# Two groups of gates and partners, and the last six feature blocks of a down product, as Strassen's seven products

## The chip, the cores and the metric

The kernel runs on one core of a Trainium2 chip. The metric is the device time of one execution in microseconds (us). The engines that matter here are TensorE (PE, the matmuls), VectorE (DVE), ScalarE (ACT) and the queue of DMA issues on SyncE (SP).

## The reference

Two decoder blocks over a sequence of 512 rows of width 1024, in float32. The first has latent and windowed attention and a plain feed-forward network, the second a convolution beside a dilated attention, and then this, which is where the change lies:

```python
    h = rmsnorm(x, g_ffn[i])
    gate = causal_dwconv3(h @ w_gate[i], ffn_conv_w[i], ffn_conv_b[i])
    x = x + (jax.nn.silu(gate) * (h @ w_up[i])) @ w_down[i]
    ple_gate = jax.nn.sigmoid(rmsnorm(x, g_ple[i]) @ w_ple_gate[i])
    x = x + ple_gate * (p[i].astype(x.dtype) @ w_ple_proj[i])
```

`w_gate` and `w_up` are 1024 x 2816 and `w_down` is 2816 x 1024. `causal_dwconv3` weighs each feature's row with the two rows before it.

## The kernel before

**Precision.** Every float32 operand is split into a rounded part `hi` (a cast on ACT) and a rest `lo` (a subtraction on DVE); `split` does both. `mm3` makes three matmuls of a pair of operands, hi·hi, hi·lo and lo·hi, into one PSUM bank. Weights come by DMA into raw tiles (`wr`, three slots, or `wq`, four) and are split into `wh` and `wl`, which have four slots of 1024 columns each. There are eight PSUM banks.

**Gates and partners.** The 2816 features are 22 blocks of 128 and 11 groups of two blocks. For a group, `gated(gr, 0)` makes the gate (banks `gp`) and `gated(gr, 1)` the partner from `w_up` (banks `up`): each 8 steps of 128 deep, two blocks, three matmuls of 128x512, 48 in all. `gate_ev` makes the convolution (ACT `y`, two dependent steps on DVE for each block) and the silu on ACT; `up_ev` multiplies with the partner. The products of groups 0 to 7 go into raw tiles `hr` (`RAW`, four blocks in one tile), those of groups 8 to 10 are split at once into `ah` and `al` (list `H`). Group 0 is made by `gated_first`, in an order that follows the arrival of the normalized tiles. Groups 1 to 3 follow, and then groups 4 to 10 stand between the products of the down calls.

**The down product.** The first 16 feature blocks go through `down_steps` in two calls of eight blocks. A call takes two raw tiles as a 2 x 2 matrix of operands (A11, A21, A12, A22) and four quarters of the weights (`wq`: B11, B22, B12, B21) and makes the seven products of the Strassen-Winograd scheme in place of eight: sums of the A's (`a_sum`), of the B's (`b_sum`), the split of each operand (`a_op` into `aop`, `b_op` into `wh`, `wl`), 24 matmuls of 512 columns per product into the banks `r`, and additions of the banks into `x` (`ev_add`). Its generator yields after every product, and a part of a gated group is made between two products.

**The last six blocks.** Blocks 16 to 21 are a plain product over 6 steps of 128: `gemm_tm` for the left half of the columns (`tm`), `gemm_tm_t` for the right (`tt`), which has 144 matmuls of 512 columns in all, and whose additions into `x` (`ev_down`) are followed, tile by tile of 128 rows, by `to_ple`: row weights `xn`, squares with a sum on ACT (`xs`), and the factor of the last norm (`rv`, `rr`, `rs`, `ra`, `ro`). `put_off` lets the transposes of `xn` (`pt` into `xth`, `xtl`) wait for a later `tick` of PE's program. The ple gate (`tt<-wh,xth`) and its sigmoid `sg` end the kernel. In front of it stands the projection of `p_2` (`pt` of `pin`, `ptp`, `tm<-wh,ptp`, copies to `pp`).

**Order.** Each engine runs its instructions in one order, which a scheduler has laid down by priorities (`tc.high_priority`, with the offsets `A_PRIO` for the A operands, `B_PRIO` for the B operands and `W_PRIO` for weights).

Of the kernel before, what the change touches and what calls it, by code (L numbers as in the profile page):

```python
# [26 lines left out]
W_PRIO = 60  # L27
# [17 lines left out]

WEAVE = (-1, -1, -1, 0, -1, 1, -1, -1, 2, -1, 3)
A_PRIO, B_PRIO = 120, 80
MLA_WO_AT = (0, 0, 21, 23)


@with_exitstack
def tile_hybrid_decoder(ctx: ExitStack, tc: tile.TileContext, io: dict, out: bass.AP):
# [195 lines left out]
    def krows(W, k0, kn, c0, n):  # L248
        return W[k0 * P:(k0 + kn) * P, c0:c0 + n].rearrange("(k p) c -> p k c", p=P)
# [339 lines left out]
    with ExitStack() as mla:  # L589
# [300 lines left out]

    ts2 = slice(0, 256), slice(256, 512)

    def down_steps(mb, wd, row, ra, rb, alpha, after=None):


        A11, A21, A12, A22 = ra[:, :, ts2[0]], ra[:, :, ts2[1]], rb[:, :, ts2[0]], rb[:, :, ts2[1]]
        B = {}
        for r, h in ((0, 0), (1, 1), (0, 1), (1, 0)):
            n_big[0] += 1
            B[r, h] = q = mb.tile([P, 4, S], F32, tag="q", name=f"wq_{n_big[0]}")  # L900
            for i in range(2):
                nc.sync.dma_start(out=q[:, 2 * i:2 * i + 2, :],
                                  in_=krows(wd, row + r * 4 + 2 * i, 2, h * 512, 512))
        B11, B12, B21, B22 = B[0, 0], B[0, 1], B[1, 0], B[1, 1]

        def a_op(src):
            o = big("aop")
            hl = o.rearrange("p k c -> p (k c)").rearrange("p (f k c) -> p f k c", f=2, k=4)
            with tc.high_priority(offset=A_PRIO):
                split(hl[:, 0], hl[:, 1], src)  # L910
            return hl

        def a_sum(out, a, b, op):
            with tc.high_priority(offset=A_PRIO):
                nc.vector.tensor_tensor(out=out, in0=a, in1=b, op=op)

        def b_sum(out, a, b, op):
            with ExitStack() as es:
                es.enter_context(tc.high_priority(offset=A_PRIO))
                if after:  # L920
                    es.enter_context(tc.issue_after(after))
                for i in range(2):
                    ks = slice(2 * i, 2 * i + 2)
                    nc.vector.tensor_tensor(out=out[:, ks, :], in0=a[:, ks, :], in1=b[:, ks, :], op=op)  # L924

        def b_op(src):
            res = []
            for i in range(2):
                n_big[0] += 1
                wh = wp.tile([P, 1024], F32R, tag="wh", name=f"wh_{n_big[0]}")  # L930
                wl = wp.tile([P, 1024], F32R, tag="wl", name=f"wl_{n_big[0]}")
                with tc.high_priority(offset=B_PRIO):
                    split(wh, wl, src[:, 2 * i:2 * i + 2, :].rearrange("p k c -> p (k c)"))
                res.append([t.rearrange("p (k c) -> p k c", k=2) for t in (wh, wl)])
            return res

        def product(R, a, b, start):
            for i, (wh, wl) in enumerate(b):
                for tb in range(2):
                    for k in range(2):  # L940
                        ts_ = slice(tb * P, (tb + 1) * P)
                        kk = 2 * i + k
                        mm3(R[tb], (a[:, 0, kk, ts_], a[:, 1, kk, ts_]), (wh[:, k, :], wl[:, k, :]),
                            start and kk == 0, kk == 3)

        def add(R, th, h, al=1.0):
            for tb in range(2):
                ev_add(x, al)(h, 2 * th + tb, R[tb])

        def banks2(n):  # L950
# [48 lines left out]
        yield  # L999

    def mlp_ln(xt_in, x, l, first, nxt, rms=False):

# [567 lines left out]
    X = xt[2]  # L1570
    wg, wu, wd = io["w_gate_2"][0], io["w_up_2"][0], io["w_down_2"][0]
    with pool("ff", 2) as ff:
        H = []

        RAW = {}
        Y = {}

# [15 lines left out]
                nc.scalar.activation(y, y, AF.Silu)  # L1593

        def up_ev(gr, banks):
            if gr < 8 and gr % 2 == 0:
                RAW[gr // 2] = big("hr", F32)
            elif gr % 2 == 0:
                hh, hl = big("ah"), big("al")
                H.extend((hh[:, m, :], hl[:, m, :]) for m in range(4 if gr < 10 else 2))  # L1600
            for m in range(2):
                if gr < 8:
                    turned["y", gr] = nc.vector.tensor_tensor(
                        out=RAW[gr // 2][:, gr % 2 * 2 + m, :], in0=Y.pop((gr, m)), in1=banks[m], op=ALU.mult).ins
                    continue
                n_big[0] += 1
                a = ff.tile([P, S], F32, tag="a", name=f"a_{n_big[0]}")
                nc.vector.tensor_tensor(out=a, in0=Y.pop((gr, m)), in1=banks[m], op=ALU.mult)
                split(*H[gr * 2 + m - 16], a)
# [155 lines left out]
```

## Time and profile before

| | us |
|---|---|
| median of 3 runs | 1692.81 (1691.04 to 1693.84) |
| profiled execution | 1690.43 |
| its span | 1688.6 |
| PE busy in it | 1669.5 |
| DVE busy | 1111.0 |
| ACT busy | 829.3 |

The span is the part of the profiled execution between the first and the last instruction. Engines work side by side; matmuls are pipelined, so the start of one to the start of the next is what one costs in a stream, and not the time between its start and its end.

### The profile page before, as it was taken

The numbers are of one execution on the slowest core, as the hardware profiler recorded it, in microseconds if no ns is written. First come the engines' busy times: TensorE is split into PE (matmuls) and PEld (weight loads), VectorE is DVE, ScalarE is ACT, GpSimd is POOL, SyncE is SP. The second block draws the span as 40 slices with busy tenths as digits, with TensorE's granted clock in tenths as the row PEclk, the third lists the DMA queues.
The fourth block names the chain that finished last, engine by engine and source line by source line (L and its number), as shares of the span: only waits on it lengthen the run. The fifth ranks groups of instructions, "written<-read, shape, count | busy, mean of one in ns | idle before, by whom it ended". The sixth has DMA issues, their size and how long they took to land.

```text
span 1688.6 us, 21336 instructions
## 1 busy us (share of the span) xinstructions
PE 1669.5 (99%) x8239; PEld 1384.7 (82%) x8239; DVE 1111.0 (66%) x1938; ACT 829.3 (49%) x1416; POOL 25.6 (2%) x43
## 2 busy tenths in 40 slices
PE   8999999999999999999999999999999999999998
PEld 8777898888888877798888888988779888888887
DVE  5876648576846578738586846556765567577463
ACT  4665445444543578445444545444854343344442
POOL 0000000000001110000000000001000000000000
PEclk9999999999999999999999999999999999999999
DMA  5213244333132323413333143133352323422321
GB/s 181 69 46 130 88 150 119 100 100 100 50 125 87 101 63 119 156 50 101 101 99 100 50 126 111 39 125 99 100 187 63 88 76 99 125 63 63 113 88 63
DMA packets 125015, 165.22 MB, mean 98 GB/s; under 512 B 9385, under 2 KB 80322, under 8 KB 124914
## 3 DMA queue, kind: packets, MB, share of 16 engines
q1 hardware_dynamic: 119072, 150.03, 28.2%
q10 hardware_dynamic: 4626, 10.94, 1.9%
q0 software_dynamic: 1216, 2.89, 0.8%
q8 instruction: 65, 1.06, 0.3%
q14 instruction: 36, 0.29, 0.1%
HBM read 160.95 MB, written 2.88 MB: 97 GB/s over the span
## 4 chain that ended last, share of the span: by engine, by line
PE 94%; DVE 3%; ACT 1%; DMA 1%; issue 0%; SPq 0%; ACTq 0%; DVEq 0%
PE up L202 8%; PE up L204 8%; PE up L203 8%; PE r L202 6%; PE r L204 6%; PE r L203 6%; PE tt L203 3%; PE tt L204 3%; PE tt L202 3%; PE tm L202 2%; PE tm L203 2%; PE fm L202 2%; PE tm L204 2%; PE fm L203 2%; PE fm L204 2%; PE gp L204 2%
## 5 line engine op out<-in xcount | busy, mean ns | idle before, releaser
L120 DVE TENSOR_TENSOR wl<-wr,wh 128x1024 fp32r<-128x1024 f32 (+5 forms) x219 | 222.8, 1032 | 168.8 <-ACT wh L119 167.7
L119 ACT CAST wh<-wr 128x1024 fp32r<-128x1024 f32 (+5 forms) x219 | 193.6, 898 | 273.1 <-PE up L203 118.0
L202 PE MATMUL up<-xth,wh 128*128 128x512 f32 x608 | 236.5, 389 | 0.0
L203 PE MATMUL up<-xtl,wh 128*128 128x512 f32 x608 | 236.5, 389 | 0.0
L204 PE MATMUL up<-xth,wl 128*128 128x512 f32 x608 | 236.5, 389 | 0.0
L120 DVE TENSOR_TENSOR wl<-wq,wh 128x1024 fp32r<-128x1024 f32 x112 | 136.4, 1223 | 101.0 <-ACT wh L119 100.9
L119 ACT CAST wh<-wq 128x1024 fp32r<-128x1024 f32 x112 | 118.0, 1054 | 159.2 <-PE r L204 82.4
L204 PE MATMUL r<-wh,aop 128*128 128x512 f32 x448 | 174.3, 389 | 0.0
L202 PE MATMUL r<-wh,aop 128*128 128x512 f32 x448 | 174.3, 389 | 0.0
L203 PE MATMUL r<-wl,aop 128*128 128x512 f32 x448 | 174.3, 389 | 0.0
L204 PEld LDWEIGHTS up<-xth,wl 128*128 128x128 f32 x608 | 114.1, 188 | 23.8
L203 PEld LDWEIGHTS up<-xtl,wh 128*128 128x128 f32 x608 | 114.1, 188 | 23.6
L202 PEld LDWEIGHTS up<-xth,wh 128*128 128x128 f32 x608 | 114.1, 188 | 23.5
L204 PEld LDWEIGHTS r<-wh,aop 128*128 128x128 f32 x448 | 84.1, 188 | 17.5
L203 PEld LDWEIGHTS r<-wl,aop 128*128 128x128 f32 x448 | 84.1, 188 | 17.4
L202 PEld LDWEIGHTS r<-wh,aop 128*128 128x128 f32 x448 | 84.1, 188 | 17.4
L885 DVE SCALAR_TENSOR_TENSOR x<-x,r 128x512 f32<-128x512 f32 x144 | 92.5, 684 | 5.4 <-PE r L204 5.4
L120 DVE TENSOR_TENSOR aop<-hr,aop 128x1024 fp32r<-128x1024 f32 x56 | 67.0, 1221 | 21.5 <-ACT aop L119 21.5
L924 DVE TENSOR_TENSOR wq<-wq,wq 128x1024 f32<-128x1024 f32 x64 | 76.2, 1223 | 6.4 <-DMA wq<-in_w_down_dram 3.9
L202 PE MATMUL gp<-xth,wh 128*128 128x512 f32 x160 | 62.3, 389 | 0.0
L203 PE MATMUL gp<-xtl,wh 128*128 128x512 f32 x160 | 62.3, 389 | 0.0
L204 PE MATMUL gp<-xth,wl 128*128 128x512 f32 x160 | 62.2, 389 | 0.0
(426 smaller groups left out, 3561.4 us busy)
## 6 DMA issues: line engine op xcount, KB each, us to landing
wr<-in_mlp_w_up_dram SPq DMA_DIRECT2D x64, 512.0 KB, 3.8
wq<-in_mlp_w_down_dram SPq DMA_DIRECT2D x48, 512.0 KB, 4.3
wr<-in_w_in_dram SPq DMA_DIRECT2D x24, 512.0 KB, 3.6
wr<-in_w_gate_dram SPq DMA_DIRECT2D x22, 512.0 KB, 3.7
wr<-in_w_up_dram SPq DMA_DIRECT2D x22, 512.0 KB, 3.6
wr<-in_mlp_w_down_dram SPq DMA_DIRECT2D x16, 512.0 KB
wq<-in_w_down_dram SPq DMA_DIRECT2D x16, 512.0 KB, 7.8
wr<-in_mla_w_o_dram SPq DMA_DIRECT2D x8, 512.0 KB, 3.7
```

What stands on the lines that cost most here:

```text
L119: turned["hi"] = nc.scalar.copy(out=hi, in_=src).ins
L120: return nc.vector.tensor_tensor(out=lo, in0=src, in1=hi.bitcast(F32), op=ALU.subtract)
L202: nc.tensor.matmul(o, lhsT=sh, rhs=mh, start=start, stop=False, skip_group_check=True)
L203: nc.tensor.matmul(o, lhsT=sh, rhs=ml, start=False, stop=False, skip_group_check=True)
L204: nc.tensor.matmul(o, lhsT=sl, rhs=mh, start=False, stop=stop, skip_group_check=True)
L885: nc.vector.scalar_tensor_tensor(out=x[:, t, cs], in0=x[:, t, cs], scalar=alpha, in1=pb, op0=ALU.mult, op1=ALU.add)
L924: nc.vector.tensor_tensor(out=out[:, ks, :], in0=a[:, ks, :], in1=b[:, ks, :], op=op)
```

## The change

Two things are remade as seven products.

`gated_seven` makes the gate and the partner of groups 2 and 3 together. The operands are the four quarters of the normalized input (two halves of the depth, two halves of the 512 rows; `x_operands` makes the sums `s1` to `s4` of them once) and, as weights, the two halves of the depth of `w_gate` (B11, B21) and of `w_up` (B12, B22), in tiles `fq`. Each product is 24 matmuls of 128x256 into one bank, whose two halves are the group's two blocks; three banks take part, and `plus` on DVE adds the banks to the parts `fp` and `fv` (tile names with f: `fg` gate, `fu` partner).

The last six blocks go through `down_steps` with three steps of depth per quarter (`nk=3`) in place of four, with the last two products in reverse order (`fin`), so that `to_ple` is called for the tiles as they are complete. The six blocks stay in raw tiles, `RAW[4]` and `RAW[5]`, so `H` and its splits are gone. The loads of the ple gate's weights (`ahead2`) are issued between the products. In every call of `down_steps` the sum and the split of `s4` now stand ahead of the split of B21.

```diff
+SEVEN = 4
...
-    def down_steps(mb, wd, row, ra, rb, alpha, after=None):
+    def down_steps(mb, wd, row, ra, rb, alpha, after=None, nk=4, fin=None):
...
-            for i, (wh, wl) in enumerate(b):
+            for k0, kn, wh, wl in b:
                 for tb in range(2):
-                    for k in range(2):
+                    for k in range(kn):
...
+            tick()
...
-        b = b_op(B21)
-        product(R3, a22, b, False)
         a_sum(A12, A12, A22, ALU.subtract)
         s4 = a_op(A12)
-        add(R3, 1, 0)
-        yield
-        b = b_op(B22)
-        product(R2, s4, b, False)
-        add(R2, 0, 1)
-        yield
+        rest = [(R3, a22, B21, 1, 0), (R2, s4, B22, 0, 1)]
+        for R, a, src, th, h in reversed(rest) if fin else rest:
+            b = b_op(src)
+            product(R, a, b, False)
+            add(R, th, h, last=True)
+            yield
...
+            G, U = tmp("g", 2), tmp("u", 2)
+            p1, v = tmp("p"), tmp("v")
+            R1, R2, R3 = bank("gt"), bank("gt"), bank("gt")
+            product(R1, B11, "a11", True)
+            nc.scalar.copy(out=p1, in_=both(R1))
+            b_sum(B12, B22, B12, ALU.subtract)
+            product(R3, B12, "s3", True)
+            plus(v, p1, R3)
+            b_sum(B11, B12, B11, ALU.add)
+            product(R2, B11, "s2", True)
+            plus(G[:, :, ts2[1]], p1, R2)
+            product(R1, B21, "a12", False)
+            nc.scalar.copy(out=G[:, :, ts2[0]], in_=both(R1))
+            b_sum(B21, B21, B11, ALU.subtract)
+            product(R3, B21, "a22", False)
+            plus(G[:, :, ts2[1]], G[:, :, ts2[1]], R3)
+            gate_ev(gr, [G[:, m, :] for m in range(2)])
+            b_sum(B11, B22, B11, ALU.subtract)
+            product(R2, B11, "s1", False)
+            plus(U[:, :, ts2[1]], v, R2)
+            product(R2, B22, "s4", False)
+            plus(U[:, :, ts2[0]], p1, R2)
+            up_ev(gr, [U[:, m, :] for m in range(2)])
...
         gated_first()
-        for gr in range(1, 4):
+        ops = x_operands()
+        gated(1, 0)
+        gated(1, 1)
+        with pool("fm", 1) as fm:
+            for gr in range(2, SEVEN):
+                gated_seven(gr, fm, ops)
+        for gr in range(SEVEN, 4):
             for part in range(2):
                 gated(gr, part)
...
-        gemm_tm(H, wd[16 * P:22 * P, :], [LO], ev_down)
-        ahead2 = gemm_tm_t(H, wd[16 * P:22 * P, :], [HI], ev_down, 1,
-                           nxt=lambda: ahead_tm(io["w_ple_gate_2"][0], 0, 512))
+        with pool("fl", 4) as fl:
+            ahead2 = Ahead([(krows(io["w_ple_gate_2"][0], k, 2, 0, 512), 2, 512, None) for k in range(0, 8, 2)])
+            for i, _ in enumerate(down_steps(fl, wd, 16, RAW.pop(4)[:, 0:3, :], RAW.pop(5)[:, 0:3, :], 1.0, nk=3,
+                                             fin=to_ple)):
+                if 2 <= i < 6:
+                    ahead2.one()
```

**DVE at the end of the groups.** In the order of before, the last product with the partner of group 3 (`hr<-y,up`) and what follows it:

```order
L1324 SCALAR_TENSOR_TENSOR y_11869<-gp_11803,vec,y_11869 128x510
L120 TENSOR_TENSOR wl_12004<-wr_12002,wh_12003 128x1024
L1603 TENSOR_TENSOR hr_11799<-y_11864,up_11874 128x512
L1603 TENSOR_TENSOR hr_11799<-y_11869,up_11875 128x512
L120 TENSOR_TENSOR wl_12034<-wr_12032,wh_12033 128x1024
L120 TENSOR_TENSOR aop_12108<-hr_11799,aop_12108 128x1024
L915 TENSOR_TENSOR hr_11799<-hr_11799,hr_11526 128x4x256
L120 TENSOR_TENSOR wl_12075<-wq_11947,wh_12074 128x1024
```

In the order of the change, the same place; `wl_12179` is the first half of the first weights of the first down call:

```order
L1671 TENSOR_TENSOR fg_11933<-fg_11933,gt_11939 128x2x256
L1325 SCALAR_TENSOR_TENSOR y_12088<-fg_11933,vec,y_12088 128x511
L1325 SCALAR_TENSOR_TENSOR y_12093<-fg_11933,vec,y_12093 128x511
L1327 SCALAR_TENSOR_TENSOR y_12088<-fg_11933,vec,y_12088 128x510
L1327 SCALAR_TENSOR_TENSOR y_12093<-fg_11933,vec,y_12093 128x510
L1671 TENSOR_TENSOR fu_11934<-fv_11936,gt_11938 128x2x256
L1671 TENSOR_TENSOR fu_11934<-fp_11935,gt_11938 128x2x256
L1602 TENSOR_TENSOR hr_11922<-y_12088,fu_11934 128x512
L1602 TENSOR_TENSOR hr_11922<-y_12093,fu_11934 128x512
L121 TENSOR_TENSOR aop_12330<-hr_11922,aop_12330 128x1024
L916 TENSOR_TENSOR hr_11922<-hr_11922,hr_11526 128x4x256
L916 TENSOR_TENSOR hr_11526<-hr_11526,hr_11922 128x4x256
```

The next row of the change is `L121 TENSOR_TENSOR wl_12179<-wq_12163,wh_12178 128x1024`. In the order of before the first two splits of that call stand seven and three rows ahead of the first row shown; now the split stands behind the last `hr`, the split of A12 and two sums.

**DVE in the tail.** Before, the splits of the last six blocks' weights, and the first additions into `x` behind them:

```order
L120 TENSOR_TENSOR wl_13719<-wr_13717,wh_13718 128x1024
L120 TENSOR_TENSOR wl_13734<-wr_13732,wh_13733 128x1024
L120 TENSOR_TENSOR wl_13740<-wr_13738,wh_13739 128x1024
L1648 TENSOR_TENSOR x_375_1792<-x_375_1792,tm_13607 128x512
L1648 TENSOR_TENSOR x_375_1792<-x_375_1792,tm_13608 128x512
L1648 TENSOR_TENSOR x_375_1792<-x_375_1792,tm_13609 128x512
```

In the change, the additions from the bank pair of the first product (`r_13835`, `r_13836`), which the fourth product takes again, and what stands ahead of them:

```order
L121 TENSOR_TENSOR aop_13972<-hr_13240,aop_13972 128x768
L121 TENSOR_TENSOR wl_13911<-wq_13812,wh_13910 128x512
L916 TENSOR_TENSOR hr_13457<-hr_13457 128x3x256
L121 TENSOR_TENSOR wl_13946<-wq_13821,wh_13945 128x1024
L121 TENSOR_TENSOR wl_13950<-wq_13821,wh_13949 128x512
L925 TENSOR_TENSOR wq_13821<-wq_13821,wq_13812 128x1024
L925 TENSOR_TENSOR wq_13821<-wq_13821,wq_13812 128x512
L925 TENSOR_TENSOR wq_13812<-wq_13815,wq_13812 128x1024
L925 TENSOR_TENSOR wq_13812<-wq_13815,wq_13812 128x512
L886 SCALAR_TENSOR_TENSOR x_375_1792<-x_375_1792,r_13835 128x512
L121 TENSOR_TENSOR wl_13986<-wq_13812,wh_13985 128x1024
L121 TENSOR_TENSOR wl_13990<-wq_13812,wh_13989 128x512
```

Six of the seven splits of A operands, the splits of the first four products' weights and the sums stand ahead of the first of the six additions; the other five come behind the last row shown.

**ACT at the end of the tail.** Before, the casts of the first transposed tile of `x` (`xth`) for the ple gate:

```order
L424 ACT_TABLE_LOAD
L424 ACTIVATE rs_13785<-rr_13784 128x1
L1642 ACTIVATE xs_13819,s_1915_13814<-x_375_1792 128x512
L424 ACTIVATE rs_13824<-rr_13823 128x1
L1642 ACTIVATE xs_13859,s_1926_13854<-x_375_1792 128x512
L119 CAST xth_13770<-pt_13873 128x4x128
```

In the change, at the same place:

```order
L1722 ACTIVATE xs_14131,s_1966_14126<-x_375_1792 128x512
L1722 ACTIVATE xs_14129,s_1966_14126<-x_375_1792 128x512
L425 ACT_TABLE_LOAD
L425 ACTIVATE rs_14065<-rr_14064 128x1
L1722 ACTIVATE xs_14149,s_1975_14146<-x_375_1792 128x512
L1722 ACTIVATE xs_14151,s_1975_14146<-x_375_1792 128x512
L120 CAST xth_14050<-pt_14167 128x4x128
```

The first cast stood ahead of the last of the eight squares, and now it stands behind all eight, two of which need the seventh product.

## Rows read from the trace of the kernel before

**Rows 1.** The page: busy time by engine; the chain that ended last.
```profile
PE 1669.5 (99%) x8239; PEld 1384.7 (82%) x8239; DVE 1111.0 (66%) x1938; ACT 829.3 (49%) x1416; POOL 25.6 (2%) x43
...
PE 94%; DVE 3%; ACT 1%; DMA 1%; issue 0%; SPq 0%; ACTq 0%; DVEq 0%
```
**Rows 2.** Waits of PE from 1250 us to the end, the longest.
```profile
PE wo L202 <- ACT yah L123: 0.8, 1, 0.8
...
```
**Rows 3.** Timeline of PE, 512-column matmuls: start, us, engine, line.
```profile
1559.14 0.39 PE L202 MATMUL gp<-xth,wh 128*128 128x512 f32 x1
...
1561.86 0.39 PE L202 MATMUL gp<-xth,wh 128*128 128x512 f32 x1
```
**Rows 4.** Windows: length, busy PE, PEld, DVE, ACT, POOL, clock, DMA share, GB/s.
```profile
4.00:8.00 4.00, 1.94 (x8) 1.57 (x8) 0.73 (x2) 1.65 (x3) 0.00 (x0) 1.00 0.92 309
...
1278.00:1296.00 18.00, 18.00 (x153) 18.00 (x152) 9.68 (x12) 8.90 (x11) 0.00 (x0) 1.00 0.39 117
1296.50:1340.00 43.50, 43.50 (x195) 36.03 (x194) 22.11 (x24) 14.48 (x17) 0.00 (x0) 1.00 0.30 83
...
1590.43:1636.61 46.18, 45.60 (x209) 37.73 (x208) 25.09 (x45) 22.33 (x41) 0.00 (x0) 1.00 0.36 117
```
**Rows 5.** Timeline of PE, 256-column matmuls.
```profile
1272.04 0.28 PE L204 MATMUL gt<-xth,awl 128*128 128x256 f32 x1
...
1273.00 0.28 PE L203 MATMUL gt<-xtl,awh 128*128 128x256 f32 x1
```
**Rows 6.** Timeline of DVE: first and last of four in a row, 1024 elements.
```profile
1319.23 1.22 DVE L924 TENSOR_TENSOR wq<-wq,wq 128x1024 f32<-128x1024 f32 x1
...
1322.63 1.22 DVE L924 TENSOR_TENSOR wq<-wq,wq 128x1024 f32<-128x1024 f32 x1
```
**Rows 7.** Groups of instructions by form: busy us, mean ns, idle before.
```profile
L119 ACT CAST wh<-wq 128x1024 fp32r<-128x1024 f32 x112 | 118.0, 1054 | 159.2 <-PE r L204 82.4 <-PE up L203 68.3 <-PE gp L203 8.5
...
L885 DVE SCALAR_TENSOR_TENSOR x<-x,r 128x512 f32<-128x512 f32 x144 | 92.5, 684 | 5.4 <-PE r L204 5.4
...
L1322 DVE SCALAR_TENSOR_TENSOR y<-gp,vec,y 128x511 f32<-128x511 f32 x20 | 15.0, 748 | 8.3 <-ACT y L1321 8.3
...
L1321 ACT ACTIVATE y<-gp,vec 128x512 f32<-128x512 f32 x20 | 15.5, 776 | 18.7 <-PE gp L204 18.7
```
**Rows 8.** Timeline of DVE in the first rms_norm of the stage.
```profile
1264.59 0.22 DVE L426 SCALAR_TENSOR_TENSOR ra<-rv,rs 128x1 f32<-128x1 f32 x1 [0.27 <-ACT rs L424]
```
**Rows 9.** Timeline of PE at the borders of the stages.
```profile
1318.42 0.39 PE L202 MATMUL gp<-xth,wh 128*128 128x512 f32 x1
...
1362.40 0.39 PE L204 MATMUL r<-wh,aop 128*128 128x512 f32 x1
...
1584.98 0.39 PE L202 MATMUL r<-wh,aop 128*128 128x512 f32 x1
...
1603.07 0.39 PE L202 MATMUL tm<-wh,ah 128*128 128x512 f32 x1
...
1643.07 0.71 PE L447 MATMUL pt<-ident,xn 128*128 128x128 f32 x5
```
**Rows 10.** Timeline of ACT during the projection.
```profile
1599.26 0.59 ACT L1681 COPY pp<-tm 128x512 f32<-128x512 f32 x1
```
**Rows 11.** Timeline of ACT: a table load before the sigmoid.
```profile
1640.47 1.28 ACT L1691 ACT_TABLE_LOAD   x1
```
**Rows 12.** The page's DMA issues: KB each, us to landing.
```profile
wq<-in_w_down_dram SPq DMA_DIRECT2D x16, 512.0 KB, 7.8
```
**Rows 13.** Timeline of PE at the start of the program: transposes.
```profile
4.75 1.94 PE L447 MATMUL pt<-ident,x 128*128 128x128 f32 x8 [4.75 <-DMA x<-in_x_dram]
8.57 1.97 PE L447 MATMUL pt<-ident,x 128*128 128x128 f32 x8 [1.88 <-DMA x<-in_x_dram]
...
10.60 1.27 PE L447 MATMUL pt<-ident,x 128*128 128x128 f32 x5
...
14.60 1.03 PE L447 MATMUL pt<-ident,x 128*128 128x128 f32 x8
```

More of the change, by code (lines that the diff above doesn't have):

```diff
@@ L899, in down_steps @@
             n_big[0] += 1
[L900 to L903, printed above, removed]
+            B[r, h] = q = mb.tile([P, nk, S], F32, tag="q", name=f"wq_{n_big[0]}")
+            for k0 in range(0, nk, 2):
+                kn = min(2, nk - k0)
+                nc.sync.dma_start(out=q[:, k0:k0 + kn, :], in_=krows(wd, row + r * nk + k0, kn, h * 512, 512))
         B11, B12, B21, B22 = B[0, 0], B[0, 1], B[1, 0], B[1, 1]
@@ L921, in b_sum @@
                     es.enter_context(tc.issue_after(after))
-                for i in range(2):
-                    ks = slice(2 * i, 2 * i + 2)
+                for k0 in range(0, nk, 2):
+                    ks = slice(k0, min(k0 + 2, nk))
                     nc.vector.tensor_tensor(out=out[:, ks, :], in0=a[:, ks, :], in1=b[:, ks, :], op=op)
@@ L927, in b_op, with add @@
             res = []
[L928 removed]
+            for k0 in range(0, nk, 2):
+                kn = min(2, nk - k0)
                 n_big[0] += 1
[L930 to L931 removed]
+                wh = wp.tile([P, 1024], F32R, tag="wh", name=f"wh_{n_big[0]}")[:, :kn * 512]
+                wl = wp.tile([P, 1024], F32R, tag="wl", name=f"wl_{n_big[0]}")[:, :kn * 512]
                 with tc.high_priority(offset=B_PRIO):
[L933 to L934 removed]
+                    split(wh, wl, src[:, k0:k0 + kn, :].rearrange("p k c -> p (k c)"))
+                res.append((k0, kn) + tuple(t.rearrange("p (k c) -> p k c", k=kn) for t in (wh, wl)))
             return res
         def product(R, a, b, start):
[L938 removed]
+            for k0, kn, wh, wl in b:
                 for tb in range(2):
[L940 removed]
+                    for k in range(kn):
                         ts_ = slice(tb * P, (tb + 1) * P)
[L942 removed]
+                        kk = k0 + k
                         mm3(R[tb], (a[:, 0, kk, ts_], a[:, 1, kk, ts_]), (wh[:, k, :], wl[:, k, :]),
[L944 to L946 removed]
+                            start and kk == 0, kk == nk - 1)
+            tick()
+        def add(R, th, h, al=1.0, last=False):
             for tb in range(2):
                 ev_add(x, al)(h, 2 * th + tb, R[tb])
+                if last and fin:
+                    fin(2 * th + tb)
         def banks2(n):
@@ L1572, in tile_hybrid_decoder @@
     with pool("ff", 2) as ff:
-        H = []
         RAW = {}
@@ L1595, in up_ev @@
         def up_ev(gr, banks):
[L1596 to L1600, printed above, removed]
-            for m in range(2):
[L1602 to L1609, printed above, removed]
+            for m in range(2):
+                M = gr * 2 + m
+                c, k = (M // 4, M % 4) if M < 16 else (4 + (M - 16) // 3, (M - 16) % 3)
+                if k == 0:
+                    RAW[c] = big("hr", F32)
+                turned["y", gr] = nc.vector.tensor_tensor(out=RAW[c][:, k, :], in0=Y.pop((gr, m)), in1=banks[m],
+                                                          op=ALU.mult).ins
         def gated(gr, part):
@@ L1615, in gated, with x_operands, op @@
             (gate_ev, up_ev)[part](gr, banks)
+        def x_operands():
+            raw = [big("xr", F32) for _ in range(2)]
+            for i in range(2):
+                for th in (0, 1):
+                    nc.vector.tensor_tensor(out=raw[i][:, :, ts2[th]], in0=xt[0][i][:, :, ts2[th]].bitcast(F32),
+                                            in1=xt[1][i][:, :, ts2[th]].bitcast(F32), op=ALU.add)
+            A11, A21, A12, A22 = [raw[i][:, :, ts2[th]] for i in range(2) for th in range(2)]
+            def op(out, a, b, how):
+                nc.vector.tensor_tensor(out=out, in0=a, in1=b, op=how)
+                o = big("xs").rearrange("p k c -> p (k c)").rearrange("p (f k c) -> p f k c", f=2, k=4)
+                split(o[:, 0], o[:, 1], out)
+                return o[:, 0], o[:, 1]
+            q = {i + 1: (xt[0][i // 2][:, :, ts2[i % 2]], xt[1][i // 2][:, :, ts2[i % 2]]) for i in range(4)}
+            ops = {"a11": q[1], "a12": q[3], "a22": q[4]}
+            ops["s3"] = op(A21, A11, A21, ALU.subtract)
+            ops["s2"] = op(A22, A22, A21, ALU.subtract)
+            ops["s1"] = op(A11, A11, A22, ALU.add)
+            ops["s4"] = op(A12, A12, A22, ALU.subtract)
+            return ops
@@ new lines, in gated_seven, with tmp, b_sum, product @@
+        def gated_seven(gr, fm, ops):
+            B = {}
+            for r in range(2):
+                for h, W in enumerate((wg, wu)):
+                    n_big[0] += 1
+                    B[r, h] = q = fm.tile([P, 4, 256], F32, tag="q", name=f"fq_{n_big[0]}", bufs=4)
+                    nc.sync.dma_start(out=q, in_=krows(W, 4 * r, 4, gr * 256, 256))
+            B11, B12, B21, B22 = B[0, 0], B[0, 1], B[1, 0], B[1, 1]
+            def tmp(name, w=1):
+                n_big[0] += 1
+                return fm.tile([P, 2, 256 * w], F32, tag=name, name=f"f{name}_{n_big[0]}")
+            def b_sum(out, a, b, how):
+                with tc.high_priority(offset=W_PRIO):
+                    nc.vector.tensor_tensor(out=out, in0=a, in1=b, op=how)
+            def product(R, B, a, start):
+                n_big[0] += 1
+                wh = wp.tile([P, 1024], F32R, tag="wh", name=f"wh_{n_big[0]}")
+                wl = wp.tile([P, 1024], F32R, tag="wl", name=f"wl_{n_big[0]}")
+                with tc.high_priority(offset=W_PRIO):
+                    split(wh, wl, B.rearrange("p k c -> p (k c)"))
+                wh, wl = (t.rearrange("p (k c) -> p k c", k=4) for t in (wh, wl))
+                ah, al = ops[a]
+                for m in range(2):
+                    for k in range(4):
+                        cs = slice(m * P, (m + 1) * P)
+                        mm3(R[:, m * 256:m * 256 + 256], (wh[:, k, cs], wl[:, k, cs]), (ah[:, k, :], al[:, k, :]),
+                            start and m == 0 and k == 0, k == 3)
+                tick()
+            def both(R):
+                return R.rearrange("p (m c) -> p m c", m=2)
+            def plus(out, a, R):
+                nc.vector.tensor_tensor(out=out, in0=a, in1=both(R), op=ALU.add)
+            G, U = tmp("g", 2), tmp("u", 2)
[21 more added lines that the diff above has]
+            up_ev(gr, [U[:, m, :] for m in range(2)])
```

7 lines of the change are left out of this document (1 added, 6 removed).

## Prediction

> **What bounds the kernel now.** I began with the page: PE is busy for 1669.5 of 1688.6 us and the chain that ended last runs through it for 94% [rows 1], so what counts is the length of PE's stream and its pauses. PE's waits after 1250 us are the next view: four short ones, the longest 0.8 us, none in the plain gate groups or the down product [rows 2]. Matmuls of 512 columns follow each other without a hole: 12 from 1559.14 to 1561.86, 0.2267 us each [rows 3]. Then the windows: over the first groups of gates DVE works 22 of 43.5 us, over the end of the down product 25 of 46 [rows 4]. That is the stock on which the change draws, since it takes columns off PE and pays with sums and splits on DVE.
>
> The profiled execution took 1690.43 us; the median of the runs is 1692.81, 2.4 above. Sums are made against the profiled one, and 2.4 is added at the end. A measurement of this kernel tells 0.2% (3.4 us) from no change.
>
> **What PE saves.** A group has 96 matmuls of 512 columns, 96 x 0.2267 = 21.76 us. By seven products it has 7 x 24 = 168 of 256 columns. Such matmuls follow each other at 0.120 us: eight steps from 1272.04 to 1273.00 [rows 5]. 168 x 0.120 = 20.16, so a group saves 1.6 us and two save 3.2. In the tail 144 matmuls of 512 become 7 x 18 = 126: 18 x 0.2267 = 4.1 us. Together 7.3 us, if PE never waits. The row of 0.120 is more than half of 0.2267. The Trainium skill (TensorE: Matmul & The Clock Gate, Back-to-back issue gap) gives N/2.4 + 2.5 ns for isolated matmuls, an estimate of 109 against 216 ns, by which two groups would save 4.8 us and not 3.2, and the sum would be 1.6 us lower; the same section says that in streams with weight loads the spacing also hangs on those, and the trace agrees (PEld busy for 18.00 of 18.00 us between 1278 and 1296, where the 256-column matmuls run).
>
> **What it adds on DVE before the first down call.** Prices: 1.14 us from start to start for 128x1024 (four from 1319.23 to 1322.63, three steps), some 0.6 to 0.7 for 512 elements [rows 6, 7]. `x_operands` adds 12 of 1024. A group of seven products gives 7 splits, 4 sums (1024), 5 `plus`, 4 convolution steps and 2 products with `up` (512): 11 x 1.14 + 11 x 0.65 = 19.7 us per 20.2 us of PE, where a plain group had 4 splits and 6 of 512, 8.5 per 21.8. With group 1 that is 38 x 1.14 + 28 x 0.65 = 61.5 us between 1296.9 and 1358.7, which is 61.8: no slack is left, so each place where DVE must wait for PE comes back as a wait of PE.
>
> One b_sum of the first seven stands, by the order, between `rr` and `ra` of the first rms_norm, in front of the transposes that PE is waiting for around 1269 [rows 8]. 1.14 less the 0.27 that DVE idles there: **+0.85** us. Bounds: 0, if a later tile sets the end there, and 1.14.
>
> The walk through the gate stage, with 2.88 us (24 x 0.120) per product from 1318.42 [rows 9]: the seven products of group 2 find their operands (the splits need 1.14 of every 2.88). In group 3 the gate is complete after the fifth product, at 1353.5. Then `fg` 0.7, ACT's `y` 0.78, four convolution steps of 0.72, and only then `fu<-fv`, which empties the bank R2 (the order piece shows the convolutions ahead of it): 1358.9 with hand-overs. The seventh product accumulates into R2 and could have begun at 1356.3: a wait of 2.6. An earlier one of 0.35 comes from the other `fu` of group 2. The seventh ends at 1361.8. Behind it the DVE rows run as one chain: `fu` 0.7, `hr`, `hr` 1.3, ACT's cast 1.05, `aop` lo 1.14, two a_sums 2.3, and then `wl` of the down call's first weights, 1.2 [rows 6, 7], with hand-overs 8.2 us: 1370.0. Before, PE waited nowhere for this `wl`. The first `r` has all it needs for its third matmul at 1370.0 where it had it at 1362.40 [rows 9]: **+7.65** net of the 3.2 saved. Bounds: -3.2, if the scheduler's chain is covered, and +10, if the 512-element steps with three-dimensional operands cost 0.9. No room is left to give back the delay later, since PE runs gapless from there.
>
> **What it adds in the tail.** Count from the last `r` block of the second call, 1584.98; the projection (`tm`) that comes next ends 18.1 later [rows 9], by me at 17.5, since one of its small waits is filled. Seven products of 18 matmuls, 4.08 us each: 17.5, 21.6, 25.7, end 29.75. The fourth accumulates into R1, and DVE must first have made the six additions from R1 into x. They stand, by the order, behind the a_ops, weight splits and b_sums of all that follows. DVE is dense from about 15.1, when ACT hands over the first `aop` cast behind the copies to `pp` [rows 10]: 9 of 768 elements (0.87, by elements between 0.6 and 1.14), 6 of 1024, 11 of 512: 7.8 + 6.8 + 6.6 = 21.2, to 36.5. The fourth product starts at 36.7: **a wait of 6.9**. Before, DVE had 25.1 us of work in these 46 us [rows 4] and PE never waited. The fifth product waits 1.5 for the additions from its bank, the sixth and seventh 3 together for a split and for R2 again, and the seventh ends at 55.9. The transposes of x then run to 56.9, but ACT's `xth` stands behind the four squares of tiles 2 and 3 (512 elements each, which add up to 3 us with their reads) and a table load of 1.28 [rows 11], by the order; that puts it at 61 and the first `tt` of the ple gate at 61.8, a wait of 5. Its 24 matmuls end at 68.3, where they ended at 58.1 (1643.07): **+10.0** with the 4.1 saved. Bounds: -4.1, and +13 if a 768 costs like a 1024.
>
> **Other edits.** In the eight down calls that stay, s4's sum and splits go ahead of B21's split: two rows change places on DVE and ACT, none on PE. Cover is the ring of four weight slots; before, PE waited nowhere for it in the two calls of this block [rows 2]; I take 0, without that cover 1 us per call. The loads: wq of the tail has six 512 KB equivalents, issued when the last `wl` of the second call is through; eight took 7.8 us median to land [rows 12], and there are 17 us. 0, or +2 if SP reaches them late.
>
> **Sum:** 0.85 + 7.65 + 10.0 = +18.5, 1708.9 in the profile's own terms at an undisturbed clock.
>
> **TensorE's clock.** At the start of the program, behind a wait of 4.75 us, PE made eight transposes in 1.94 and again in 1.97 us, which later took 1.03, and five in 1.27, at the later price 0.64 [rows 13]. Durations double as at 1.2 GHz instead of 2.4, though the granted clock in the row of that stretch reads 1.00 [rows 4]. Loss: 0.91 + 0.94 + 0.63 = 2.5 us. Behind the short waits after 1250 us [rows 2] no stretch reads below 1.00. The change makes waits of 6.9, 5 and (with two matmuls in between) 8 us; I take one such loss, for the longest unbroken wait, **+2.5**: 1711.4, and 1713.8 with the 2.4: forecast **1714**, by itself 1707 to 1720.
>
> **Rivals.**
> 1. *Every long wait halves the clock behind it.* Three losses of 2.5: 1708.9 + 7.5 + 2.4 = 1719. For it speaks the start of the program, against it that PE was never busy before that wait, so it may not have fallen at all. The Trainium skill (TensorE: Matmul & The Clock Gate, What's actually happening) states it as a rule: idle brings the half rate, and work releases it; no wait inside the trace of before is long enough to show whether it does. Chance 0.20.
> 2. *One of the two delays is hidden.* If the additions from R1 are made in time, the tail saves 4.1: 1692.8 + 0.85 + 7.65 - 4.1 = 1697. If the chain behind the last product of group 3 is hidden, the stage saves 3.2: 1692.8 + 0.85 - 3.2 + 10 = 1700.5. It needs DVE to run some 7 us ahead of my walk. Chance 0.13.
> 3. *DVE keeps its lead (faster).* Mechanism: in both places the rows ahead of the decisive one are done when their inputs come, since DVE was busy only 66% over the span, and PE's stream gets 7.3 us shorter: 1685.5. It decides if `wl` of the first down weights is done by 1358.7, before its product could start, and the R1 additions by 29.7 in the tail; my walk has them 11 and 7 us later. DVE runs strictly by its order in each row I read, which speaks against it. Chance 0.12.
> 4. Half of one delay alone, within 0.2%: 0.05. The forecast has 0.50.
>
> **How the numbers follow.** Forecast 0.50, rivals 0.20, 0.13, 0.12, 0.05. Slower: 0.50 + 0.20 + 0.13 = 0.83; same 0.05; faster 0.12. The range for 8 in 10 starts at 1697, the lower of rival 2's times, leaves out rival 3 and the same, and reaches to 1724, rival 1 with the tail's upper bound partly paid.
>
> **What would show it.** In the profile after: a wait of PE's `r` on DVE's `wl` of some 4 to 8 us between 1360 and 1372; `gt` waiting 2 to 3 us for `fu`; in the tail an `r` that waits some 7 us for DVE's x, and `tt` that waits some 5 for ACT's `xth`; `tt`'s first 24 matmuls some 18 to 21 us later than 1643. Wrong it is if PE shows no wait over 2 us there, or if 256-column matmuls run at 0.109 or at 0.14.

## The result and the profile after

The changed kernel took 1716.65 us (1714.35 to 1718.33) where the kernel before took 1693.05 beside it: a ratio of 1.014, 95% interval 1.0123 to 1.0158. A second measurement, with more executions, gave 1716.69 against 1691.32, 1.0152 (1.0138 to 1.0166), that is 25.4 us slower. The profiled execution of the first took 1718.33 us; its span is 1716.1, 27.5 above that of before.

The page after, to be held against [rows 1] (same columns):

```profile
PE 1673.0 (97%) x8365; PEld 1392.2 (81%) x8365; DVE 1169.0 (68%) x2005; ACT 847.1 (49%) x1439; POOL 25.6 (1%) x43
...
PE 88%; DVE 6%; ACT 2%; DMA 2%; issue 1%; SPq 0%; ACTq 0%; DVEq 0%
```

PE is busy longer, not shorter, although it has fewer columns to stream, and DVE and ACT now hold 8% of the chain that ended last. The waits of PE from 1240 us on say where (what waited, for whom: us in total, times, longest); in [rows 2] the longest was 0.8:

```profile
PE r L203 <- DVE x L886: 6.9, 1, 6.9
PE tt L203 <- ACT xth L120: 4.6, 1, 4.6
PE r L203 <- ACT wh L120: 4.2, 1, 4.2
PE r L204 <- DVE wl L121: 3.5, 2, 2.7
PE gt L203 <- ACT y L1594: 2.4, 1, 2.4
PE gt L203 <- DVE fu L1671: 1.6, 1, 1.6
PE pt L448 <- DVE xn L491: 1.5, 1, 1.5
```

The row of 2.4 names the silu on ACT (`y`), which ended at 1362.74. By the program the seventh product waits for its bank, which DVE's `fu<-fv` had emptied at 1362.62; PE began at 1362.77. Both stand behind the same convolution steps on DVE.

Then the windows around them (columns as in [rows 4]; the last number but two is the granted clock):

```profile
1360.00:1370.00 10.00, 4.63 (x28) 4.16 (x26) 4.60 (x7) 2.10 (x3) 0.00 (x0) 0.83 0.22 63
1370.00:1380.00 10.00, 6.05 (x13) 4.29 (x14) 9.69 (x9) 5.04 (x6) 0.00 (x0) 0.56 0.84 305
1380.00:1390.00 10.00, 10.00 (x42) 8.16 (x41) 9.23 (x12) 3.15 (x3) 0.00 (x0) 0.93 0.33 100
...
1662.00:1669.00 7.00, 6.61 (x21) 5.26 (x22) 3.32 (x18) 1.79 (x6) 0.00 (x0) 0.56 0.00 0
```

The granted clock reads 0.56 to 0.93 of 2.4 GHz in the windows behind the waits, a mean over stretches at 1.2 and at 2.4 GHz. The timeline of PE shows the step, in the middle of the seventh product of group 3, 1.5 us after a wait of 2.4 had ended (start, us, engine, line):

```profile
1364.04 0.28 PE L204 MATMUL gt<-xs,wh 128*128 128x256 f32 x1
1364.16 0.28 PE L205 MATMUL gt<-xs,wl 128*128 128x256 f32 x1
1364.28 0.38 PE L203 MATMUL gt<-xs,wh 128*128 128x256 f32 x1
1364.45 0.42 PE L204 MATMUL gt<-xs,wh 128*128 128x256 f32 x1
1364.67 0.42 PE L205 MATMUL gt<-xs,wl 128*128 128x256 f32 x1
...
1371.20 1.22 PE L203 MATMUL r<-wh,aop 128*128 128x512 f32 x2 [4.20 <-ACT wh L120]
1375.17 0.79 PE L204 MATMUL r<-wl,aop 128*128 128x512 f32 x1 [2.75 <-DVE wl L121]
1375.76 0.63 PE L205 MATMUL r<-wh,aop 128*128 128x512 f32 x1
...
1380.88 0.63 PE L203 MATMUL r<-wh,aop 128*128 128x512 f32 x1
1381.31 0.43 PE L204 MATMUL r<-wl,aop 128*128 128x512 f32 x1
1381.58 0.40 PE L205 MATMUL r<-wh,aop 128*128 128x512 f32 x1
```

Starts stand 0.12 apart and then 0.21; in the first product of `r` 0.43 apart, and 0.23 again from 1381.58. Up to 1364.2 the 256-column matmuls ran at the 0.120 of [rows 5].

The chain on DVE behind the last product of group 3, in DVE's timeline (the first row stands ahead of that product and empties its bank): from 1367.04 on each row starts as the one before it ends, but for the cast on ACT (1.11).

```profile
1361.94 0.68 DVE L1671 TENSOR_TENSOR fu<-fv,gt 128x512 f32<-128x512 f32 x1
1367.04 0.69 DVE L1671 TENSOR_TENSOR fu<-fp,gt 128x512 f32<-128x512 f32 x1 [4.42 <-PE gt L205]
1367.83 1.29 DVE L1602 TENSOR_TENSOR hr<-y,fu 128x512 f32<-128x512 f32 x2
1370.24 1.23 DVE L121 TENSOR_TENSOR aop<-hr,aop 128x1024 fp32r<-128x1024 f32 x1 [1.11 <-ACT aop L120]
1371.50 2.48 DVE L916 TENSOR_TENSOR hr<-hr,hr 128x1024 f32<-128x1024 f32 x2
1373.90 1.22 DVE L121 TENSOR_TENSOR wl<-wq,wh 128x1024 fp32r<-128x1024 f32 x1
```

The third matmul of `r` starts at 1375.17, where it started at 1362.40 [rows 9]. In the tail, DVE's timeline has the additions behind splits and sums, and ACT's has the cast behind squares and a table load:

```profile
1629.16 3.56 DVE L925 TENSOR_TENSOR wq<-wq,wq 128x1024 f32<-128x1024 f32 x4
1632.63 0.68 DVE L886 SCALAR_TENSOR_TENSOR x<-x,r 128x512 f32<-128x512 f32 x1
1633.30 1.83 DVE L121 TENSOR_TENSOR wl<-wq,wh 128x1024 fp32r<-128x1024 f32 x2
1635.05 3.07 DVE L886 SCALAR_TENSOR_TENSOR x<-x,r 128x512 f32<-128x512 f32 x5
```
```profile
1659.14 1.28 ACT L425 ACT_TABLE_LOAD   x1
1660.44 0.20 ACT L425 ACTIVATE rs<-rr 128x1 f32<-128x1 f32 x1
...
1661.78 0.56 ACT L120 CAST xth<-pt 128x512 fp32r<-128x512 f32 x1
```

The five additions end at 1638.1. The fourth product writes to the two banks that they empty, the first bank first, and so starts a little ahead of that end; the next row is the ple gate's first product:

```profile
1637.67 0.77 PE L203 MATMUL r<-wh,aop 128*128 128x512 f32 x1 [6.86 <-DVE x L886]
...
1662.39 0.80 PE L203 MATMUL tt<-awh,xth 128*128 128x512 f32 x1 [4.60 <-ACT xth L120]
```

### The profile page after: what moved, and what is told of

It is laid out like the page before. It is cut to its first block, busy times and chain, and to the rows that moved or that the text cites. A ratio compares the mean times of both kernels' runs of the same rounds, so it can differ in the third digit from the quotient of the medians.

```text
span 1716.1 us, 21707 instructions
## 1 busy us (share of the span) xinstructions
PE 1673.0 (97%) x8365; PEld 1392.2 (81%) x8365; DVE 1169.0 (68%) x2005; ACT 847.1 (49%) x1439; POOL 25.6 (1%) x43
## 4 chain that ended last, share of the span: by engine, by line
PE 88%; DVE 6%; ACT 2%; DMA 2%; issue 1%; SPq 0%; ACTq 0%; DVEq 0%
PE up L205 8%; PE up L204 8%; PE up L203 8%; PE r L204 6%; PE r L205 6%; PE r L203 6%; PE tt L204 2%; PE tt L203 2%; PE tt L205 2%; PE fm L203 2%; PE fm L204 2%; PE fm L205 2%; PE tm L203 2%; PE tm L204 2%; PE tm L205 2%; PE gp L204 2%
## 5 line engine op out<-in xcount | busy, mean ns | idle before, releaser
L120 ACT CAST wh<-wr 128x1024 fp32r<-128x1024 f32 (+5 forms) x201 | 174.8, 884 | 248.6 <-PE up L204 112.3
L121 DVE TENSOR_TENSOR wl<-wr,wh 128x1024 fp32r<-128x1024 f32 (+5 forms) x201 | 201.0, 1015 | 139.3 <-ACT wh L120 138.5
L121 DVE TENSOR_TENSOR wl<-wq,wh 128x1024 fp32r<-128x1024 f32 x126 | 149.4, 1192 | 98.7 <-ACT wh L120 98.6
L203 PE MATMUL r<-wh,aop 128*128 128x512 f32 x490 | 192.8, 394 | 11.1 <-DVE x L886 6.9
L204 PE MATMUL r<-wl,aop 128*128 128x512 f32 x490 | 192.6, 393 | 3.5 <-DVE wl L121 3.5
L205 PE MATMUL r<-wh,aop 128*128 128x512 f32 x490 | 192.2, 393 | 0.0
L203 PEld LDWEIGHTS r<-wh,aop 128*128 128x128 f32 x490 | 93.0, 190 | 31.2 <-issue 7.2
L205 PEld LDWEIGHTS r<-wh,aop 128*128 128x128 f32 x490 | 93.1, 190 | 19.5
L121 DVE TENSOR_TENSOR aop<-hr,aop 128x1024 fp32r<-128x1024 f32 (+1 forms) x63 | 73.4, 1191 | 22.8 <-ACT aop L120 22.8
L120 ACT CAST aop<-hr 128x1024 fp32r<-128x1024 f32 (+1 forms) x63 | 62.5, 1023 | 10.0 <-DVE hr L1602 6.4
L203 PE MATMUL fm<-xth,wh 128*128 128x256 f32 (+1 forms) x192 | 61.4, 320 | 0.2 <-ACT xth L120 0.2
L204 PE MATMUL fm<-xtl,wh 128*128 128x256 f32 (+1 forms) x192 | 61.0, 318 | 0.0
```

The lines of the kernel that those rows point to most:

```text
L203: nc.tensor.matmul(o, lhsT=sh, rhs=mh, start=start, stop=False, skip_group_check=True)
L204: nc.tensor.matmul(o, lhsT=sh, rhs=ml, start=False, stop=False, skip_group_check=True)
L205: nc.tensor.matmul(o, lhsT=sl, rhs=mh, start=False, stop=stop, skip_group_check=True)
```

## The experiments

Differences are between the medians of a kernel and of the kernel before on the same chip. For the changed kernel this is 25.4 us (the run told last); the first measurement gave 23.6, so a gain told below is known to some 2 us, and the traces have to say what became of the waits.

**One part alone: the groups.**

```diff
         with pool("fm", 1) as fm:
             for gr in range(2, SEVEN):
                 gated_seven(gr, fm, ops)
...
+        gemm_tm(H, wd[16 * P:22 * P, :], [LO], ev_down)
+        ahead2 = gemm_tm_t(H, wd[16 * P:22 * P, :], [HI], ev_down, 1,
+                           nxt=lambda: ahead_tm(io["w_ple_gate_2"][0], 0, 512))
-        with pool("fl", 4) as fl:
...
```

> Groups 2 and 3 by seven products, the last six blocks as before. Theory (each place has its own delay: DVE behind the last product of group 3 in the stage, the additions from R1 and the order of ACT in the tail): the stage's part alone, +1.4 at the rms norm and +12.9 from group 2 to the first r block, 1693 + 14 = 1707, and the long wait of r in the tail is gone. Rival (one delay, shared: the tail is late because the stage left DVE behind): nearly all of the 24 us stay, 1713 or more, or nearly none, 1696 or less.

1705.45 against 1691.08, +14.4 (ratio 1.0086, interval 1.0072 to 1.01).

**The other part alone: the tail.**

```diff
-        ops = x_operands()
-        gated(1, 0)
-        gated(1, 1)
-        with pool("fm", 1) as fm:
-            for gr in range(2, SEVEN):
-                gated_seven(gr, fm, ops)
-        for gr in range(SEVEN, 4):
+        for gr in range(1, 4):
```

> All groups of gates as before, the last six blocks by seven products. Theory: the tail's part alone, +12.6: 1693 + 12.6 = 1705.6, with r's wait of 6.9 us for the additions and tt's of 4.6 for the cast where they are in the changed kernel. Rival (shared): under 1697, since DVE comes to the tail without the backlog of the stage.

1702.38, +11.3 (1.0067, 1.0053 to 1.0081). The two make 25.7, and both together 25.4, so the delays add up. The trace of the groups alone has the waits of 2.4, 4.2 and 2.7 and no long one in the tail, that of the tail alone has those of 6.9 and 4.6 and no long one in the stage. A shared delay is ruled out.

**The order of s4 alone.**

```diff
-        b = b_op(B21)
-        product(R3, a22, b, False)
         a_sum(A12, A12, A22, ALU.subtract)
         s4 = a_op(A12)
+        b = b_op(B21)
+        product(R3, a22, b, False)
         add(R3, 1, 0)
```

> The kernel before with only the sum and the splits of s4 ahead of the split of B21 in all down calls. Theory: no change, 1693 within 0.1%; the 1.2 us by which the changed kernel is late before the second block's gates is the scatter of executions. Rival: those 1.2 us are the reorder's, 1694 to 1695.

1691.22, +0.1 (1.0003, 0.9994 to 1.0011): no change, as forecast.

**Waits filled with matmuls that no one reads.** `fill` was called around the last product of group 3, before the tail's fourth product and before the ple gate's first.

```diff
+    def fill(o, st, mv, n):
+        for _ in range(n):
+            nc.tensor.matmul(o, lhsT=st[:, 0:P], rhs=mv, start=True, stop=True, skip_group_check=True)
...
+            if gr == 3:
+                fill(R1, X[0][0], X[0][0], 7)
             product(R2, B22, "s4", False)
+            if gr == 3:
+                fill(R1, X[0][0], X[0][0], 33)
```

> The changed kernel with matmuls that no one reads in PE's four long waits (12 and 28 of 512 columns around the last product of group 3, 28 before the fourth product of the tail, 18 before the first product of the ple gate), so that PE isn't idle there. Theory (the half clock is an effect of the waits and costs some 8 us in all: 1.0 and 3.0 in the stage, 1.4 and 2.8 in the tail): granted clock 1.00 throughout, 512-column matmuls 0.227 apart behind the waits, 1716.7 - 7 = 1710 or so. Rival (the clock falls for another reason, or costs nothing because DVE sets the pace anyway): 1716 or slower.

In the edit the two fills of group 3 are 7 and 33 matmuls, not 12 and 28.

1714.71, +23.6. The run decides nothing: its condition for the last place also held in the first block, where the trace has 18 such matmuls around 1050 us, over 4 us of PE's time. Without them:

> The changed kernel with matmuls that no one reads in PE's four long waits only (the run before it, e4_fill, had 18 of them in the first block too, about 4.5 us that belong to no wait). Theory (the half clock behind the waits costs some 7 to 8 us by itself): clock 1.00 throughout, some 17 us over the kernel before where the change alone has 23.6. Rival (it costs nothing, DVE sets the pace): 23 or more over the kernel before.

1710.74 against 1691.19, +19.5 (1.0113, 1.0098 to 1.0129), 5.8 less than the changed kernel, with the same work on DVE and ACT and 86 matmuls more on PE. The windows of this run, in the places where the clock had fallen:

```profile
1360.00:1370.00 10.00, 10.00 (x57) 8.75 (x56) 5.36 (x8) 3.27 (x4) 0.00 (x0) 1.00 0.27 73
1370.00:1380.00 10.00, 8.64 (x39) 6.83 (x38) 9.93 (x10) 4.44 (x5) 0.00 (x0) 1.00 0.82 287
...
1657.00:1667.00 10.00, 10.00 (x51) 8.32 (x50) 6.38 (x27) 3.54 (x7) 0.00 (x0) 1.00 0.01 2
```

The granted clock stays at 1.00 when PE has something to do, so the half rate is an effect of the waits and has a price of its own. The Trainium skill (TensorE: Matmul & The Clock Gate, What's actually happening) states the rule, idle brings half rate and work releases it; the trace agrees (0.56 behind the waits, 1.00 where they are filled).

**The additions of the tail ahead of the splits.**

```diff
-                ev_add(x, al)(h, 2 * th + tb, R[tb])
+                with tc.high_priority(offset=A_PRIO if fin else 0):
+                    ev_add(x, al)(h, 2 * th + tb, R[tb])
```

> The changed kernel with the additions of the tail's products into x at the priority of the A operands, so that on DVE those from R1 and R3 stand ahead of the splits for the third product. Theory (the fourth product waits for the additions only because they stand behind those splits and sums): r's wait of 6.9 us is gone and in its place the third product waits 2 us for its own split, since DVE is dense there; the tail ends 4 to 6 us earlier, 18 to 20 over the kernel before. Rival (DVE's work as a whole sets the tail, the order doesn't matter): less than 2 us gained.

1711.35, +20.2 (1.0116, 1.0099 to 1.0133), 5.2 gained. The wait for the additions is gone; PE waits 1.2 for the third product's `wl` (2 were forecast) and, not forecast, 4.6 later on for a split of A:

```profile
1628.01 0.50 PE L204 MATMUL r<-wl,aop 128*128 128x512 f32 x1 [1.23 <-DVE wl L121]
1640.20 0.79 PE L203 MATMUL r<-wh,aop 128*128 128x512 f32 x1 [4.61 <-ACT aop L120]
```

So the order of DVE decided the place of the wait and part of its length.

**A cover for the chain of the groups.**

```diff
                     for part in range(2):
-                        next(ds, None)
+                        if c or gr > 4 or part:
+                            next(ds, None)
                         gated(gr, part)
```

> The changed kernel with the gate half of group 4 moved ahead of the first product of the first down call, so that 10.9 us of PE's work lie between the last product of group 3 and the first r. Theory (the chain fu, hr, cast, split, two sums, split of the first weights has nothing to hide behind): both waits of r there (4.2 and 2.7 us) and the half clock behind them (3.0) are gone, a gain of 9 to 10: 14 over the kernel before. Rival (the weights' DMA, which starts only as the tiles of the groups come free, is what ends last): under 4 us gained, r still waits.

1703.71, +12.5 (1.0072, 1.0057 to 1.0087), 12.9 gained, the largest effect of any edit. The wait of 2.4 before the seventh product has gone too. DVE's `fu<-fv` comes no earlier; but in PE's order 13 matmuls of group 4's gate (`gp`) now stand in front of the seventh product, so the piece covers this chain as well:

```profile
1358.81 0.40 PE L203 MATMUL gp<-xth,wh 128*128 128x512 f32 x1
...
1361.79 0.27 PE L203 MATMUL gt<-xs,wh 128*128 128x256 f32 x1
```

What PE still waits for in the stage:

```profile
PE gt L203 <- DVE fu L1671: 1.2, 1, 1.2
PE r L204 <- DVE wl L121: 1.0, 2, 0.6
```

The longer of the two waits for `wl` lies in the tail. Neither is for the weights' DMA, the rival.

**The casts of the tail ahead of the squares.** `to_ple` leaves the squares and the norm's factor to a function that runs behind the transposes; `xn` and the casts and splits of the transposed tiles get a higher priority (120).

```diff
...
-            put_off(("xt", t), lambda: put_t(xt2[0], xn, t), TURN_PLE)
+            put_off(("xt", t), lambda: turned_ple(xn, t), TURN_PLE)
+
+        def turned_ple(xn, t):
+            put_t(xt2[0], xn, t, 120)
...
```

> The changed kernel with the squares and the norm's factor of the tail's tiles of x moved behind their transposes, and the casts and splits of the transposed tiles at high priority. The order then has six table loads on ACT there in place of two. Theory (the cast waits only because it stands behind eight squares and a table load): tt's wait falls from 4.6 us to 1 or 2 and the half clock behind it (2.8) is gone, 6 gained, 17 to 18 over the kernel before. Rival (xn on DVE or the transposes end later anyway): under 2 us gained.

1712.17, +21.0 (1.0127, 1.0109 to 1.0144), 4.4 gained, where 6 were forecast; by time alone it isn't clear of noise, since the interval overlaps that of the changed kernel (1.0138 to 1.0166). tt's wait fell from 4.6 to 0.5, in two pieces, and one of 0.9 for `xtl` came. The squares and roots now alternate with the sigmoid, and ACT has eight table loads of 1.28 between 1640 and 1700 (six were counted beforehand).

**Versions of each part that should not wait.** The groups with the cover and with every `b_sum` of the groups held back until the product of group 0 (`tc.issue_after(turned["y", 0])`), tail as before; and the tail with the additions and casts of above and this, groups as before (`project` makes one half of the projection):

```diff
...
             for i, _ in enumerate(down_steps(fl, wd, 16, RAW.pop(4)[:, 0:3, :], RAW.pop(5)[:, 0:3, :], 1.0, nk=3,
                                              fin=to_ple)):
-                if 2 <= i < 6:
+                if i < 2:
+                    project(i)
+                elif i < 6:
                     ahead2.one()
```

> Groups 2 and 3 by seven products and the last six blocks as before, with the gate half of group 4 as cover (as in e7_cover) and the first sum of the groups' weights held back until after the first group, out of the rms norm. Theory (what the stage costs is its chain without cover and the sum in the norm; PE's stream itself is 3.2 us shorter): 1 to 2 us under the kernel before, with a wait of some 1.3 us for fu left. Rival (DVE's extra work costs PE in other places): 1 or more over it.

1690.36 against 1691.44, -1.1 (0.9995, 0.9986 to 1.0004): not told from no change, as the theory's 1 to 2 us could hardly be. The 14.4 us of this part are gone. One wait of 1.4 for `fu` is the longest left.

> All groups of gates as before, the last six blocks by seven products, with the additions at high priority (e6_adds), the casts ahead of the squares (e8_cast), and the two halves of the projection of p between the first three products of the tail, where they stood ahead of all seven. Theory (the seven products cost only because they follow each other on PE faster than DVE can split, add and sum for them; spread over the 11 us of the projection they don't): the waits of 6.9 and 4.6 us and the half clock behind them are gone, the tail is 0 to 4 us shorter than the plain one: 1687 to 1691 beside 1691. Rival (DVE and ACT are full in the tail whatever the order): 1696 or more, with a new wait of 3 us or more.

1694.68, +3.2 (1.002, 1.0011 to 1.0029): between theory and rival. The long waits and the half clock are gone, 8 us of the 11.3, but the saving of 4.1 us doesn't come out. PE still waits 2.0 for `wl`, 1.3 and 0.8 for `aop`, and 1.7 in shorter pieces; that is 5.8 in the tail, where before had 0.6, and so more than the saving. The rest of the 3.2 isn't accounted for. Between these waits DVE, the fourth column, is full:

```profile
1596.00:1606.00 10.00, 10.00 (x45) 8.21 (x46) 9.27 (x16) 5.66 (x9) 0.00 (x0) 1.00 0.01 2
1606.00:1616.00 10.00, 10.00 (x46) 8.28 (x45) 10.00 (x12) 7.63 (x11) 0.00 (x0) 1.00 0.14 52
1616.00:1626.00 10.00, 10.00 (x45) 7.95 (x43) 9.88 (x13) 7.41 (x12) 0.00 (x0) 1.00 0.19 55
```

> Both parts of the change with all the edits of e9_gates_cover and e10_down_weave. Theory (the two places are independent): the sum of their two differences, 1 to 6 us under the kernel before. Rival: over it.

1693.63, +2.2 (1.0016, 1.0007 to 1.0025), the sum of -1.1 and +3.2. The theory's gain failed with the tail's; that the places are independent held.

**The changed kernel once more.**

> The changed kernel once more, unedited, for a narrower difference to the kernel before, beside which e1_gates, e2_down and e5_fill are read. Theory (the two parts add up, and the half clock costs 5 to 7 us): 23 to 26 us over the kernel before, near the sum of the two parts (14.4 and 11.3). Rival (the parts share a cost, and the filled waits gave little): 21 or less.

1716.69 against 1691.32, +25.4 (1.0152, 1.0138 to 1.0166).

## Why the prediction was right, point by point

Forecast 1714, measured 1716.65; by difference, 21.0 was forecast, 23.6 and 25.4 were measured. The mechanisms were the forecast's, two chains on DVE and ACT without cover. The span of the profiled execution, 27.5 longer, divides so (us):

| | forecast | found |
|---|---|---|
| scatter ahead of the norm | | 1.2 |
| the sum in the norm | 0.85 | 1.3 |
| the stage, from group 2 to the first `r` | 7.65 | 9.3 |
| the tail | 10.0 | 7.4 |
| the half clock | 2.5 | 8.2 |

The borders are the start of group 2, 1318.42 before, and of the last `r` block of the second call, 1584.98 before [rows 9]; the last three rows of "found" are taken with the half clock as counted below:

```profile
1320.93 0.28 PE L203 MATMUL gt<-xth,wh 128*128 128x256 f32 x1
...
1600.80 0.39 PE L203 MATMUL r<-wh,aop 128*128 128x512 f32 x1
```

At an undisturbed clock the terms make 18.0, where 18.5 were worked out. That this is so near is in part luck: norm and stage are 2.1 above their terms, the tail 2.6 below its own.

- **PE's saving.** 256-column matmuls ran at 0.120, as taken. In time the saving of the groups isn't shown: covered, they are 1.1 us under the kernel before, which is not told from no change.
- **The sum in the norm**, +0.85 expected. PE's first `gt` came at 1273.68 and not 1270.81; 1.2 us of the difference stood there before the norm and are scatter (e7_cover and e8_cast, with the same program up to there, lack them), so some 1.7 are the norm's, of which 1.3 are left at the start of group 2. What was missed: with `ra` late, the next tile's addition into x goes in front of `ro` and `xn`. The bound of 1.14 was too low.
- **The waits for `fu`**, 0.35 and 2.6 expected, 1.6 and 2.4 found. The first is longer because DVE waited 2.2 us at 1337 for the DMA of group 3's weights, which the walk left out; in e12_again DVE waits 1.7 there and PE 1.2, both shorter by 0.45.
- **The chain to the first r**, 8.2 expected: from the last matmul of group 3, which started at 1366.6, to 1375.17 it is 8.6. Over the whole stage the third matmul of `r` is 12.8 late, 2.5 of it before group 2: 10.3, where 7.65 were forecast; 1.0 of the rest is the half clock in the seventh product (11 matmuls, 0.09 each) and 1.3 the longer wait. That the place was right is shown by the cover, which took 12.9 us off.
- **The tail.** The wait for the additions is 6.9, as forecast, and the one for the cast 4.6 (5). For the later products the prediction names waits of 1.5 and 3, but its end of 55.9 holds only 2.9 of them (36.7 and four products of 4.08 make 53.0); 0.8 came. These two make up the 2.6 by which the term was too high. The sign of `tt`, its first 24 matmuls 18 to 21 late, came out at 28.5: 8.2 are the half clock, 1.2 the scatter and 0.8 transposes that now stand in front of their end.
- **The clock.** One loss of 2.5 us was taken, for the longest wait alone; that step failed, since the other long waits brought one too, as rival 1 had it. Counted in the trace: 11 matmuls of the seventh product at 0.09 (1.0), some 14 of `r` at 0.2 (2.9), 7 in the tail (1.5 with the slower first), 12 of `tt` with transposes (2.8), together 8.2; in the execution of e12_again 6.7. By time, the filled waits gave 5.8. This is the term that was mis-sized, and rival 1's 1719 is as near to the measured time as 1714.
- **The other edits.** The order of s4 cost nothing, as forecast. What the loads of the tail's weights cost wasn't tested by itself; DVE's first sum in the tail waits 2.4 us for them, at 1601, and DVE pauses again, for ACT, before its dense stretch from 1616 on.

Rival 2 (one delay hidden) and rival 3 (DVE keeps its lead) did not occur: each part alone is slower by its own amount.

## What to carry to other kernels

Seven products for eight take an eighth off TensorE's stream at most and pay with sums, splits and additions on the other engines, so first count those per product: in the tail DVE was busy 9.3 to 10 of 10 us, and with every long wait gone the short ones still took more than the 4.1 us saved. Whether another order could win them isn't shown. In a dense stretch read the order of the paying engine, not its busy share: two thirds busy over the span hid two places where it was late by 7 us. A stage that ends in a chain across engines wants a piece of independent matmul work behind it; moving one such piece was worth some 11 to 13 us here, against the two measurements of the changed kernel.

## What the runs showed of the hardware that was not expected

The same wait did not always bring the half clock. Before the seventh product of group 3 PE waited 2.4 us in each of five executions with this order. In the profiled one of the changed kernel (above) 12 matmuls behind the wait ran 0.12 apart and the next 11 ran 0.21 apart; in e1_gates it was much the same. In e12_again, the same kernel once more, and in e8_cast all 24 ran 0.12 apart:

```profile
1362.43 0.35 PE L203 MATMUL gt<-xs,wh 128*128 128x256 f32 x1 [2.38 <-ACT y L1594]
...
1365.13 0.28 PE L204 MATMUL gt<-xs,wh 128*128 128x256 f32 x1
1365.25 0.28 PE L205 MATMUL gt<-xs,wl 128*128 128x256 f32 x1
```

In e6_adds the first ones were slow and the last ones fast again:

```profile
1363.10 0.42 PE L204 MATMUL gt<-xs,wh 128*128 128x256 f32 x1
1363.32 0.42 PE L205 MATMUL gt<-xs,wl 128*128 128x256 f32 x1
...
1366.88 0.28 PE L205 MATMUL gt<-xs,wl 128*128 128x256 f32 x1
```

So some 1 us of the half clock's price differs between executions of one kernel. The waits of 1.1 to 1.7 us around 1344 were followed by no slow matmul. And the granted clock in the rows read 0.56 behind the long waits, whereas at the start of the program it read 1.00 while the durations were doubled [rows 4, 13]: there the durations have to be read, not the clock.
